# Square-sums moved from ScalarE to VectorE in every third block of an RMS-norm with SiLU

## The chip, the cores and the metric

The kernel runs on one core of a Trainium2 chip. The metric is device time in microseconds (us) of one execution; lower is better. A run also leaves a profile of one execution, whose span is about 2 us shorter than the device time.

## The reference

```python
x      # [8, 1024, 2048] float32
gamma  # [2048] float32
rms = np.sqrt(np.mean(x ** 2, axis=-1, keepdims=True) + eps)
out = gamma * x / rms
return (out * (1 / (1 + np.exp(-out)))).astype(np.float32)
```

The input of 67.1 MB is read once and an output of the same size is written once.

## The kernel before

The 8192 rows are taken in 16 blocks. A block is 4 MB: 128 partitions, each with J = 4 rows of 2048 numbers. Six buffers hold blocks; a block is loaded, worked on in place, and stored from the same buffer. Loads are issued from ScalarE's queue, stores from SyncE's.

```python
def sums(b, after_first=()):
    ss = small.tile([P, J], f32, name="ss")
    na = J // 2                                   # the line that is changed
    for j in range(na, J):
        nc.vector.tensor_tensor_reduce(           # L67: square-sum of row j on VectorE
            out=junk_v, in0=row(b, j), in1=row(b, j), scale=1.0, scalar=0.0,
            op0=ALU.mult, op1=ALU.add, accum_out=ss[:, j:j + 1])
    for j in range(na):
        nc.scalar.activation(out=junk_a, in_=row(b, j), func=ACT.Square,   # L71: the same on ScalarE
                             accum_out=ss[:, j:j + 1])
        if j == 0:
            for s in after_first:
                load(s)                           # L55: a later block's load
    rms = small.tile([P, J], f32, name="rms")
    nc.scalar.activation(out=rms, in_=ss, func=ACT.Sqrt, scale=1.0 / d, bias=eps_t)   # L77
    ...

def finish(b, halves=False):
    for j in range(J):
        nc.vector.scalar_tensor_tensor(...)       # L87: row j times 1/rms times gamma
        if j % 2:
            ...
            nc.scalar.activation(..., func=ACT.Silu)   # L91: two rows at once
            if halves:
                nc.sync.dma_start(...)            # L93: half a store, last block only

for b in range(1, last - 1):                      # blocks 0 and 1 come ahead of this loop
    sums(b + 1, after_first=[b + 3] if BUFS <= b + 3 < nblk else [])
    finish(b)
    store(b)                                      # L96
    invert(b + 1)                                 # L82
finish(last - 1)
store(last - 1)
sums(last)
invert(last)
finish(last, halves=True)
```

## Time and profile before

| | before |
|---|---|
| device time, median of 3 runs | 317.31 us (317.24 to 317.36) |
| VectorE (DVE) busy | 223.6 us, 71% of the span |
| ScalarE (ACT) busy | 223.7 us, 71% |
| moved by DMA | 134.24 MB, 426 GB/s over the span |

The page's chain of work that ended last, by engine and then by line, and two of its groups of instructions (operation, what is written and read, count; busy us, mean ns of one; idle before, and what ended it):

```profile
DMA 65%; DVE 18%; ACT 10%; issue 2%; DVEq 1%; ACTq 0%
DMA xt<-in_x_dram 65%; DVE xt L87 13%; ACT xt L91 6%; DVE junk_v L67 4%; ACT junk_a L71 2%; ACT L77 2%; DVEq L161 1%; ACT L91 0%; ACT rms L77 0%; DVE rstd L82 0%; DVE ss L67 0%; DVEq L67 0%; ACTq L77 0%
...
L67 DVE CUSTOM_DVE_ANT_0 junk_v<-xt 128x2048 f32<-128x2048 f32 x32 | 73.6, 2299 | 56.6 <-DMA xt<-in_x_dram 55.9
L71 ACT ACTIVATE junk_a<-xt 128x2048 f32<-128x2048 f32 x32 | 60.1, 1879 | 26.7 <-DMA xt<-in_x_dram 26.2
```

Two thirds of the chain are loads on their way, and both groups of square-sums, the work that the change moves, stand idle mainly until a load lands. The chain can't show that the DMA engines are full; the DMA row of the page does.

### The profile page before, as it was taken

The numbers are of one execution on the slowest core, as the hardware profiler recorded it, in microseconds if no ns is written. First come the engines' busy times: TensorE is split into PE (matmuls) and PEld (weight loads), VectorE is DVE, ScalarE is ACT, GpSimd is POOL, SyncE is SP. The second block draws the span as 40 slices with busy tenths as digits, with TensorE's granted clock in tenths as the row PEclk, the third lists the DMA queues.
The fourth block names the chain that finished last, engine by engine and source line by source line (L and its number), as shares of the span: only waits on it lengthen the run. The fifth ranks groups of instructions, "written<-read, shape, count | busy, mean of one in ns | idle before, by whom it ended". The sixth has DMA issues, their size and how long they took to land.

```text
span 315.1 us, 438 instructions
## 1 busy us (share of the span) xinstructions
PE 2.1 (1%) x8; PEld 0.5 (0%) x8; DVE 223.6 (71%) x147; ACT 223.7 (71%) x144; POOL 0.2 (0%) x4
## 2 busy tenths in 40 slices
PE   0200000000000000000000000000000000000000
PEld 0000000000000000000000000000000000000000
DVE  0679499999295692957939488493984929994920
ACT  1357958999768677686676776766867668779550
POOL 0000000000000000000000000000000000000000
DMA  8999999999999999999999999999999999999997
GB/s 334 408 458 408 391 458 408 458 408 458 408 459 408 459 408 453 412 458 412 453 412 453 420 445 424 445 420 445 428 437 428 441 433 433 441 424 441 424 418 314
DMA packets 4762, 134.24 MB, mean 426 GB/s; under 512 B 532, under 2 KB 532, under 8 KB 536
## 3 DMA queue, kind: packets, MB, share of 16 engines
q10 hardware_dynamic: 2304, 67.11, 49.8%
q1 hardware_dynamic: 2456, 67.12, 49.4%
q14 instruction: 2, 0.02, 0.0%
HBM read 67.12 MB, written 67.11 MB: 426 GB/s over the span
## 4 chain that ended last, share of the span: by engine, by line
DMA 65%; DVE 18%; ACT 10%; issue 2%; DVEq 1%; ACTq 0%
DMA xt<-in_x_dram 65%; DVE xt L87 13%; ACT xt L91 6%; DVE junk_v L67 4%; ACT junk_a L71 2%; ACT L77 2%; DVEq L161 1%; ACT L91 0%; ACT rms L77 0%; DVE rstd L82 0%; DVE ss L67 0%; DVEq L67 0%; ACTq L77 0%
## 5 line engine op out<-in xcount | busy, mean ns | idle before, releaser
L87 DVE SCALAR_TENSOR_TENSOR xt<-xt,rstd,g 128x2048 f32<-128x2048 f32 x64 | 146.2, 2347 | 0.1
L91 ACT ACTIVATE xt<-xt 128x4096 f32<-128x4096 f32 x32 | 115.5, 3616 | 39.2 <-DVE xt L87 39.2
L67 DVE CUSTOM_DVE_ANT_0 junk_v<-xt 128x2048 f32<-128x2048 f32 x32 | 73.6, 2299 | 56.6 <-DMA xt<-in_x_dram 55.9
L71 ACT ACTIVATE junk_a<-xt 128x2048 f32<-128x2048 f32 x32 | 60.1, 1879 | 26.7 <-DMA xt<-in_x_dram 26.2
L77 ACT ACT_TABLE_LOAD x15 | 19.2, 1283 | 9.9 <-DVE ss L67 9.9
L91 ACT ACT_TABLE_LOAD x15 | 19.2, 1283 | 0.3
L82 DVE RECIPROCAL rstd<-rms 128x4 f32<-128x4 f32 x16 | 2.8, 173 | 10.8 <-ACT rms L77 10.8
L111 DVE COPY g<-junk_v 128x2048 f32<-128x2048 f32 x1 | 2.3, 2292 | 9.3 <-PE junk_v L109 9.3
L71 ACT ACTIVATION_READ_ACCUMULATOR junk_a<-xt 128x1 f32 x32 | 6.0, 186 | 0.0
L77 ACT ACTIVATE rms<-ss,eps_t 128x4 f32<-128x4 f32 x16 | 4.8, 297 | 1.3 <-DVE ss L67 1.1
L67 DVE DVE_READ_ACCUMULATOR2_ANT ss<- 128x1 f32 x32 | 4.5, 141 | 0.0
L104 ACT ACT_TABLE_LOAD x1 | 1.3, 1283 | 3.8 <-issue 3.8
L109 PE MATMUL junk_v<-grow,ones 1*128 1x512 f32 x8 | 2.1, 1132 | 8.1 <-DMA grow<-in_gamma_dram 8.1
L102 DVE MEMSET ones<- 128x128 f32 x1 | 0.2, 165 | 0.8 <-PEq L147 0.8
L109 PEld LDWEIGHTS junk_v<-grow,ones 1*128 1x128 f32 x8 | 0.5, 306 | 8.1 <-issue 8.1
L104 ACT ACTIVATE junk_a<-ones 128x1 f32<-128x1 f32 x1 | 0.2, 175 | 0.0
L147 POOL MEMSET const-bfloat16-1.0<- 128x1 bf16 x1 | 0.1, 101 | 0.0
L147 POOL MEMSET const-uint8-127<- 128x1 uint8 x1 | 0.1, 101 | 0.0
L147 POOL MEMSET const-float32-0.0<- 128x1 f32 x1 | 0.1, 98 | 0.2 <-issue 0.2
L147 POOL MEMSET const-float32-1.0<- 128x1 f32 x1 | 0.1, 98 | 0.0
L103 DVE MEMSET eps_t<- 128x1 f32 x1 | 0.1, 59 | 0.0
## 6 DMA issues: line engine op xcount, KB each, us to landing
xt<-in_x_dram ACTq DMA_DIRECT2D x16, 4096.0 KB, 38.7
out_dram<-xt SPq DMA_DIRECT2D x15, 4096.0 KB, 34.6
out_dram<-xt SPq DMA_DIRECT2D x2, 2048.0 KB, 9.0
grow<-in_gamma_dram SPq DMA_DIRECT2D x1, 8.0 KB
```

Source lines behind the costliest of these rows:

```text
L67: nc.vector.tensor_tensor_reduce(out=junk_v, in0=row(b, j), in1=row(b, j), scale=1.0, scalar=0.0, op0=ALU.mult, op1=ALU.add, accum_out=ss[ ...
L71: nc.scalar.activation(out=junk_a, in_=row(b, j), func=ACT.Square, accum_out=ss[:, j:j + 1])
L77: nc.scalar.activation(out=rms, in_=ss, func=ACT.Sqrt, scale=1.0 / d, bias=eps_t)
L82: nc.vector.reciprocal(out=rstd, in_=rmss.pop(b))
L87: nc.vector.scalar_tensor_tensor(out=row(b, j), in0=row(b, j), scalar=rstds[b][:, j:j + 1], in1=g, op0=ALU.mult, op1=ALU.mult)
L91: nc.scalar.activation(out=blocks[b][:, cols], in_=blocks[b][:, cols], func=ACT.Silu)
L102: nc.vector.memset(ones, 1.0)
L104: nc.scalar.activation(out=junk_a[:, 0:1], in_=ones[:, 0:1], func=ACT.Square)
L109: nc.tensor.matmul(junk_v[:, c * w:(c + 1) * w], ones[k:k + 1, :], grow[k:k + 1, :], start=True, stop=True)
L111: nc.vector.tensor_copy(out=g, in_=junk_v)
L147: nc = _bacc.Bacc("TRN2", target_bir_lowering=False, num_devices=1)
L161: with _tile.TileContext(nc) as tc:
```

## The change

VectorE takes three of the four square-sums in blocks 2, 5, 8, 11 and 14, and ScalarE one. It relieves ScalarE, which also carries the table loads, the SiLU and the issue of loads.

```diff
         ss = small.tile([P, J], f32, name="ss")
-        na = J // 2
+        na = 1 if b % 3 == 2 else 2
         for j in range(na, J):
```

## The prediction

> **What bounds the kernel now.** I read the busy shares of the page first, then its 40 slices, then the waits, and last the timeline of the end of the span. The page:
>
> ```profile
> span 315.1 us, 438 instructions
> PE 2.1 (1%) x8; PEld 0.5 (0%) x8; DVE 223.6 (71%) x147; ACT 223.7 (71%) x144; POOL 0.2 (0%) x4
> ...
> DMA  8999999999999999999999999999999999999997
> ...
> HBM read 67.12 MB, written 67.11 MB: 426 GB/s over the span
> ```
>
> Neither VectorE nor ScalarE is full: both are at 71%, and evenly loaded. The DMA row is 9 in every slice but the first and the last. Between 66 and 240 us the windows view gives a DMA share of 1.00 at 434 GB/s. The 134.24 MB of the program at 434 GB/s take 309.3 us; the other 5.8 us of the span are starting and landing. The span is that of moving bytes, and the change moves none.
>
> The waits say the same from the other side:
>
> ```profile
> DVE junk_v L67 <- DMA xt<-in_x_dram: 55.9, 11, 5.5
> ACT xt L91 <- DVE xt L87: 39.2, 28, 3.6
> ACT junk_a L71 <- DMA xt<-in_x_dram: 26.2, 11, 7.9
> ```
>
> (Columns: us in total, times, longest.) From block 5 to block 14 VectorE stands 5.5 us in front of each block's square-sums until the block has landed. That is the room that the change may fill for nothing. How far ahead the two queues run is in the page's list of issues:
>
> ```profile
> xt<-in_x_dram ACTq DMA_DIRECT2D x16, 4096.0 KB, 38.7
> out_dram<-xt SPq DMA_DIRECT2D x15, 4096.0 KB, 34.6
> ```
>
> Blocks follow each other every 19.36 us (the square-sums of block 13 start at 240.28, those of block 14 at 259.66 by the timeline). A load takes 38.7 us from issue to landing, so it stands a whole block (19.3 us) behind another load; a store takes 34.6 us and stands 15.2 us in its queue. A store issued some us later therefore still finds its queue full.
>
> Two stretches are different. At the start the engines run without waiting for loads; at the end VectorE and ScalarE run one chain up to the last store. The end, by the timeline:
>
> ```profile
> 259.66 2.30 DVE L67 CUSTOM_DVE_ANT_0 junk_v<-xt 128x2048 f32<-128x2048 f32 x1 [5.54 <-DMA xt<-in_x_dram]
> ...
> 264.27 9.13 DVE L87 SCALAR_TENSOR_TENSOR xt<-xt,rstd,g 128x2048 f32<-128x2048 f32 x4
> ...
> 300.39 4.86 SPq L93 DMA_DIRECT2D out_dram<-xt  x2
> 301.27 3.62 ACT L91 ACTIVATE xt<-xt 128x4096 f32<-128x4096 f32 x1 [0.91 <-DVE xt L87]
> ```
>
> Block 14 lands at 259.55. From there: its sums, the scaling of blocks 13 and 14, the sums of 15, its scaling, and two half stores issued at 300.39 and 304.90. The reader is to see that this chain hangs on the landing of block 14, and that block 14 is a changed block (14 mod 3 = 2).
>
> **What the Trainium skill says.** "DMA: Bandwidth & Descriptors", section "Where 436 GB/s comes from", gives 435 GB/s as the fabric ceiling of a core's DMA; the trace has 434 in mid-span, so it agrees and nothing is left to win there. The same page, "Issuing engines are not separate DMA queues", says that transfers issued from different engines run on the same 16 DMA engines and interleave: the trace agrees, with 33.52 MB of loads and 33.55 MB of stores between 85 and 240 us. "VectorE: DVE Perf Modes", section "The TRN2 errata", gives (N+151)/0.96 ns for an fp32 tensor-tensor add, 2291 ns at 2048; the square-sum here measures 2299. "ScalarE: Activation LUTs", section "What ACT_TABLE_LOAD costs", gives 186 + 0.833 N ns for an ACTIVATE with immediate scale and bias, 1892 at 2048, and 1283 for a table load; the trace has 1879 and 1283.
>
> **The change part by part.** Blocks 2, 5, 8, 11 and 14 are changed; block 15 is not. In each, one square-sum goes from ScalarE to VectorE.
> - VectorE gains 5 x (2299 + 141) ns = 12.2 us of busy time and reaches 235.8 us (75%). Start to start a square-sum costs 2.39 us (259.66 to 262.05), since its accumulator read overlaps: 5 x 2.39 = 12.0 us of engine time.
> - ScalarE loses 5 x (1879 + 186) ns = 10.3 us and falls to 213.4 us (68%).
> - The listing of instruction order shows 31 table loads on ScalarE, as before, and nothing moved on the queue of stores.
>
> Where these lie:
> - Blocks 5, 8, 11: VectorE's wait of 5.5 us becomes 3.1 for the following block. The store behind is issued 2.4 us later, with 15.2 us in hand. Worth 0.
> - Block 2, at the start. VectorE has no wait there. Its sums run from 38.35 to 43.10; then block 1 is scaled and its last SiLU ends at 55.75, where store 1 is issued. All of that moves by 2.39 us, to 58.14. But the store queue is empty there: store 0 landed at 56.2 (32.69 + 23.5), and the first large packets of store 1 appear at about 59. While no stores run, loads have the whole rate instead of half: in the extra 2.39 us they gain 2.39 x 434/2 KB/ns = 0.52 MB, which at the shared rate of 217 GB/s is 2.39 us again. So I expect blocks 5 to 15 to land 2.4 us **earlier**, and stores of blocks 1 and after to land as much later. No byte is lost.
> - Block 14, at the end: one more square-sum, +2.39 us on the chain to the last stores. Set against the earlier landing (257.2), the chain from 264.3 on stands where it stood: 2.39 - 2.39 = 0. The last two stores are issued at about 300.4 and 304.9 again.
>
> Sum: 0. Saved ScalarE time is worth nothing: no path that sets the end passes through the sums it loses (in block 14 the chain runs over VectorE's).
>
> If the landing doesn't come earlier, the last stores are issued at 302.8 and 307.3. In the trace the first packets of the half store issued at 300.39 appear at 303.25, when store 14's large packets have just ended; an idle queue starts moving about 0.9 us after an issue (first load: 0.73 to about 1.6). So the margin is 303.25 - 300.39 - 0.9, about 2.0 us, and of 2.39 some 0.4 us would show, at most about 1.5 if starting takes 2 us there.
>
> **The rivals.**
> - The end of the span takes the full price of block 14's extra sum: +2.4 us (0.8%), 319.7. For it: that sum is on the chain of waits. Against: the DMA is busy to the end (shares 0.91 to 1.08 from 290 to 313 us), so the last stores queue for their turn.
> - VectorE becomes the bound. Against: per changed block it needs about 4 x 2.30 + 3 x 2.39 + 0.2 = 16.5 us of the 19.36.
> - A new wait in the issue of loads: load b+3 needs store b-3 landed. Store 3 landed at 118.2 and load 9 was issued at 124.0; loads 2.4 us earlier and stores 2.4 later leave 1.0 us of 5.8. If negative, ScalarE stands a little in front of an issue; the load still has a whole load ahead of it, so 0.
> - Faster, because ScalarE is relieved or the engines better balanced: they were even before and neither bounds. 0 at best, some tenths from noise of DMA packing.
>
> **Range and chances.** Before is 317.31 us, its three runs within 0.12. I add 0.1 for the chance of a small hole before the last stores: 317.4 us. The range, 316.9 to 318.3, goes from an unlikely gain of 0.4 to a hole of 1. A gain of 2% is 6.3 us, more than all of the span's 5.8 us outside the transfer: not possible. A loss of 2% needs over 6 us on the chain at the end, which gets 2.4. Chances: faster 0.003, same 0.985, slower 0.012.
>
> **What would show it right or wrong.** In the changed profile VectorE at about 236 us and ScalarE at about 213; DMA row unchanged; VectorE's total wait for loads down from 55.9 to about 42 to 50; blocks 5 to 14 landing about 2.4 us earlier (block 14 at 257.2, not 259.55); last stores issued near 300.4 and 304.9. It would be wrong if the last stores came 2.4 us later and the DMA row showed a gap before them, if a wait of ScalarE's queue for stores grew to more than a block's time, or if the rate in mid-span changed with the mix of loads and stores.

## The result, and the profile after

| | before | after |
|---|---|---|
| median of 6 runs each | 317.29 us (317.21 to 317.36) | 317.18 us (316.91 to 318.33) |
| VectorE busy | 223.6 us | 235.3 us |
| ScalarE busy | 223.7 us | 213.3 us |

The ratio of after to before is 1.0001, 95% interval 0.9986 to 1.0016: the same. A ratio here is the mean time of one kernel's fast runs over that of the other's of the same rounds, so not quite the ratio of the medians above.

The page after, head and DMA row:

```profile
span 315.6 us, 438 instructions
...
PE 2.1 (1%) x8; PEld 0.5 (0%) x8; DVE 235.3 (75%) x157; ACT 213.3 (68%) x134; POOL 0.2 (0%) x4
...
DMA  8999999999999999999999999999999999999997
```

Ten instructions left ScalarE and ten came to VectorE (five square-sums, each with its accumulator read), and the DMA row is the one of before. The waits after (us in total, times, longest):

```profile
DVE junk_v L67 <- DMA xt<-in_x_dram: 44.4, 11, 5.5
ACT xt L91 <- DVE xt L87: 39.2, 28, 3.6
ACT L77 <- DVE ss L67: 23.7, 11, 5.3
ACT junk_a L71 <- DMA xt<-in_x_dram: 19.0, 7, 8.0
```

VectorE's wait for loads fell from 55.9 to 44.4 us, by 11.5: about what five square-sums of 2.39 us take. ScalarE only exchanged work for waiting: it stands 23.7 us for VectorE's sums ahead of the square root's table load, where it stood 9.9, and gave up 10.4 us of busy time. So the work moved into one engine's idle time and left idle time on the other.

The begin of block 5 before, and then four moments of the timeline after: block 5, block 14 (its first square-sum, then the scaling of block 13) and the last stores (columns: start, duration, engine, line, operation):

```profile
85.39 2.30 DVE L67 CUSTOM_DVE_ANT_0 junk_v<-xt 128x2048 f32<-128x2048 f32 x1 [5.52 <-DMA xt<-in_x_dram]
```

```profile
83.37 2.30 DVE L67 CUSTOM_DVE_ANT_0 junk_v<-xt 128x2048 f32<-128x2048 f32 x1 [1.27 <-DMA xt<-in_x_dram]
...
257.69 2.30 DVE L67 CUSTOM_DVE_ANT_0 junk_v<-xt 128x2048 f32<-128x2048 f32 x1 [5.54 <-DMA xt<-in_x_dram]
...
264.70 9.14 DVE L87 SCALAR_TENSOR_TENSOR xt<-xt,rstd,g 128x2048 f32<-128x2048 f32 x4
...
300.81 4.86 SPq L93 DMA_DIRECT2D out_dram<-xt  x2
```

Block 5 is begun at 83.37, where before it was 85.39. Block 14 is begun at 257.69, where before it was 259.66: 1.97 us earlier. Its one more square-sum costs 2.4 us, and the last stores are issued at 300.81 instead of 300.39. They land 9.0 us after their issue, as before.

### The profile page after: what moved, and what is told of

It is laid out like the page before. It is cut to its first block, busy times and chain, and to the rows that moved or that the text cites. A ratio compares the mean times of both kernels' runs of the same rounds, so it can differ in the third digit from the quotient of the medians.

```text
span 315.6 us, 438 instructions
## 1 busy us (share of the span) xinstructions
PE 2.1 (1%) x8; PEld 0.5 (0%) x8; DVE 235.3 (75%) x157; ACT 213.3 (68%) x134; POOL 0.2 (0%) x4
## 3 DMA queue, kind: packets, MB, share of 16 engines
q1 hardware_dynamic: 2456, 67.12, 49.4%
## 4 chain that ended last, share of the span: by engine, by line
DVE 43%; DMA 41%; ACT 9%; issue 3%; DVEq 1%; another core or an unknown queue 0%; ACTq 0%
DMA xt<-in_x_dram 41%; DVE xt L87 27%; DVE junk_v L67 15%; ACT xt L91 6%; ACT junk_a L71 1%; ACT L77 1%; DVEq L161 1%; DVE ss L67 0%; ACT rms L77 0%; DVE rstd L82 0%; DVEq L67 0%; ACTq L77 0%
## 5 line engine op out<-in xcount | busy, mean ns | idle before, releaser
L67 DVE CUSTOM_DVE_ANT_0 junk_v<-xt 128x2048 f32<-128x2048 f32 x37 | 85.0, 2298 | 45.1 <-DMA xt<-in_x_dram 44.4
L71 ACT ACTIVATE junk_a<-xt 128x2048 f32<-128x2048 f32 x27 | 50.6, 1875 | 19.4 <-DMA xt<-in_x_dram 19.0
L77 ACT ACT_TABLE_LOAD x15 | 19.2, 1283 | 23.8 <-DVE ss L67 23.7
L67 DVE DVE_READ_ACCUMULATOR2_ANT ss<- 128x1 f32 x37 | 5.2, 141 | 0.0
L71 ACT ACTIVATION_READ_ACCUMULATOR junk_a<-xt 128x1 f32 x27 | 5.0, 186 | 0.0
```

The costliest lines, as they stand in the source:

```text
L67: nc.vector.tensor_tensor_reduce(out=junk_v, in0=row(b, j), in1=row(b, j), scale=1.0, scalar=0.0, op0=ALU.mult, op1=ALU.add, accum_out=ss[ ...
```

## The experiments

Eleven kernels were run; all gave the reference's result. The four of the first group ran on one chip, five rounds each.

**The changed kernel again.** No edit.

> The changed kernel once more, on the chip of its parts, for its spread. Both theories: 317.2 us, ratio to before within 0.4% of 1; the last two stores issued near 300.8 and 305.3 as in its first trace, or up to 1 us around it, since its six runs spread over 1.4 us and those of before over 0.15.

Measured: 317.2 us median, but 316.82 to 320.72, against 317.13 to 317.49 of before (9 runs); ratio 0.9998 (0.9985 to 1.0012). The run of 320.72 was the profiled one, so its trace can be read; it is taken up at the end of this section. The expectation on the spread was too narrow.

**Block 2 alone.**

```diff
-        na = J // 2
+        na = 1 if b == 2 else 2
```

> Only block 2 is changed. Theory (store 1 comes 2.4 us later into an empty store queue, so loads gain that time): block 5 lands about 2.0 us earlier than before (near 83.3, not 85.3), block 14 near 257.6, and the last two stores are issued about 2 us earlier than before (298.4 and 302.9); the time stays within 0.3 us of 317.3 because the DMA has the same bytes to move. Rival (the early landing comes from elsewhere in the change, or from chance): block 14 lands at 259.5 as before, last store at 304.9.

Measured: 317.05 us, ratio 0.9999 (0.9986 to 1.0011). The timeline has block 14 begun 3.5 us earlier than before (256.18 against 259.66), and the last stores issued at 296.92 and 301.4:

```profile
256.18 2.30 DVE L67 CUSTOM_DVE_ANT_0 junk_v<-xt 128x2048 f32<-128x2048 f32 x1 [5.52 <-DMA xt<-in_x_dram]
...
296.92 4.86 SPq L93 DMA_DIRECT2D out_dram<-xt  x2
```

They land 12.4 us after issue instead of 9.0. A block has landed when the last of the 16 DMA engines is done with it. By the packet records (explained below) the median engine ended load 14 2.4 us earlier than before (255.17 against 257.56 us), as expected; the last engine ended it 3.5 us earlier (255.72 against 259.18), since the engines lie closer together in this trace. So block 2 by itself brings all later blocks forward, by more than expected, and the time stays: the stores only stand longer in their queue.

**Blocks 5, 8 and 11 alone.**

```diff
-        na = J // 2
+        na = 1 if b in (5, 8, 11) else 2
```

> Only blocks 5, 8 and 11 are changed. Theory: nothing moves: block 14 lands at 259.5, last stores issued at 300.4 and 304.9, VectorE's wait for loads down by about 7 us in total to 49, time 317.3 within 0.2. Rival (the mix of work in mid-span shifts landings or the DMA's rate): landings off by over 0.5 us.

Measured: 317.0 us, ratio 0.9994 (0.9981 to 1.0006). Block 14 is begun at 260.06, 0.4 us later than in the trace of before, and the last stores are issued 0.4 later; VectorE's wait for loads is 49.4 us in total. As the theory had it: the middle part fills a wait.

**Block 14 alone.**

```diff
-        na = J // 2
+        na = 1 if b == 14 else 2
```

> Only block 14 is changed. Theory: block 14 lands at 259.5 as before, the last two stores are issued 2.39 us later (302.8 and 307.3), of which the queue hides about 2.0: time longer by 0.4 us, at most 1.5. Rival 1 (the end pays the full price): longer by 2.4 us, 319.7. Rival 2 (hidden wholly): 317.3.

Measured: 316.97 us, ratio 0.9992 (0.9979 to 1.0004). The last stores:

```profile
302.64 4.86 SPq L93 DMA_DIRECT2D out_dram<-xt  x2
```

They are issued 2.25 us later than before and land 6.7 us after issue instead of 9.0: at the same moment. The extra sum is hidden to within 0.1 us: by the packet records the engines stand idle 0.08 us on average, 0.2 at most, before these stores, so this delay is about the whole reserve. Rival 2 was right here, and the 0.4 us of the theory were not there.

**Block 14, with two sums repeated.** How much does the end hide? The next four kernels ran on one chip, three rounds each.

```diff
-        na = J // 2
-        for j in range(na, J):
+        na = 1 if b == 14 else 2
+        for j in [*range(na, J)] + ([3, 3] if b == 14 else []):
```

> Only block 14 is changed, and VectorE does two of its square-sums of row 3 again there (same result), so the chain at the end is 3 x 2.39 = 7.2 us longer and no more bytes move. The run with one extra sum hid all of its 2.39 us. Theory (the store queue hides what it has in hand, about 2.4 us, and no more): last stores issued 7.2 us later (307.6 and 312.1), time longer by 7.2 - 2.4 = 4.8 us, 322.0 (321.3 to 322.8), with a hole in the DMA row before the last stores. Rival 1 (the end is free of VectorE): 317.2. Rival 2 (full price): 324.4.

Measured: 320.55 us, ratio 1.0111 (1.0092 to 1.0131). Busy time in three stretches near the end (PE, PEld, DVE, ACT and POOL, then clock, DMA share and GB/s):

```profile
301.00:303.00 2.00, 0.00 (x0) 0.00 (x0) 2.00 (x2) 0.03 (x1) 0.00 (x0) 1.00 1.22 524
303.00:307.00 4.00, 0.00 (x0) 0.00 (x0) 4.00 (x2) 3.59 (x1) 0.00 (x0) 1.00 0.00 0
307.00:309.00 2.00, 0.00 (x0) 0.00 (x0) 0.46 (x1) 1.50 (x1) 0.00 (x0) 1.00 0.94 393
```

From 303 to 307 no byte moves while VectorE and ScalarE work: this is the hole that the small change didn't make. The last stores are issued at 306.61, 6.2 us later than before (block 14 landed 0.9 us earlier in this trace); the span is 3.6 us longer. So about 2.6 us are hidden and the rest is paid. The time lies below the expected 321.3 to 322.8; the early landing and the somewhat larger reserve account for most of it. Both rivals fall.

**Block 2, with two sums repeated.**

```diff
-        na = J // 2
-        for j in range(na, J):
+        na = 1 if b == 2 else 2
+        for j in [*range(na, J)] + ([3, 3] if b == 2 else []):
```

> Only block 2 is changed, with the same two repeated sums, so store 1 is issued 7.2 us later than before (near 62.9). Theory: loads have the empty store queue's share for that time, blocks land earlier (block 14 by 5 to 8 us, at 252 to 254.5 instead of 259.5), and the time stays at 317.2 within 0.6, since bytes bound it. Rival (delay at the start is passed on to the end, or the later stores hold up the issue of loads so that the load queue runs dry): block 14 lands no earlier than before, time over 319.

Measured: 317.25 us, ratio 1.0001 (0.9984 to 1.0018). Block 14 is begun at 253.86, 5.8 us earlier than before, and the last two stores land 15.9 us after issue. (The trace is of a run of 318.1 us, the slowest of the four.) A delay of 7.2 us at the start costs nothing. It does make a new wait, the one named as a rival in the prediction, by the waits of this run:

```profile
DVE junk_v L67 <- DMA xt<-in_x_dram: 43.5, 9, 5.5
ACT junk_a L71 <- DMA out_dram<-xt: 37.7, 7, 5.4
```

ScalarE stands before seven blocks until a store has landed and its buffer is free for the next load; that too is hidden.

**Three sums on VectorE in every block.**

```diff
-        na = J // 2
+        na = 1
```

> VectorE takes three square-sums in every block: VectorE busy 223.6 + 16 x 2.44 = 262.7 us (83%), ScalarE 223.7 - 16 x 2.07 = 190.6. Per block VectorE needs 9.13 + 3 x 2.39 + 0.2 = 16.5 of 19.36 us. Theory: still the DMA's time, 317.2 within 0.6. Rival (balance matters): longer by the 33 us of moved work's excess or some part, over 319.

Measured: 322.17 us (321.88 to 323.12), ratio 1.0157 (1.0139 to 1.0175). The theory failed. The page:

```profile
PE 2.1 (1%) x8; PEld 0.5 (0%) x8; DVE 260.9 (81%) x179; ACT 190.9 (60%) x112; POOL 0.2 (0%) x4
...
DMA  8999999999999999999999999999999999999995
```

VectorE still waits for loads, 25.1 us in all. The DMA row is as full as before, with a share of 1.00 between 110 and 250 us, and yet 427 GB/s are moved there instead of 432. The same bytes take longer.

**Four sums on VectorE in blocks 2 to 14.**

```diff
-        na = J // 2
+        na = 0 if 2 <= b <= 14 else 2
...
+        if na == 0:
+            for s in after_first:
+                load(s)
         rms = small.tile([P, J], f32, name="rms")
```

> VectorE takes all four square-sums in blocks 2 to 14, and the load is issued ahead of the square root instead of after ScalarE's first sum. VectorE needs 9.13 + 4 x 2.39 + 0.2 = 18.9 us per block of 19.36: it can't make good what it loses at the start (3 blocks x 4.8 us = 14.3). Theory: VectorE works without a break from block 2 on and becomes the bound: scaling of block 13 ends near 284 instead of 273.4, last store near 315 instead of 304.9, time 317.2 + 10.4 - 2.4 = 325 (322 to 327). Rival (DMA still hides it): 317.2 within 1.

The edit also moves the issue of the later load ahead of the square root, since ScalarE has no sum left behind which to issue it. Measured: 320.6 us (319.9 to 322.5), ratio 1.0112 (1.0076 to 1.0147); the trace is of the run of 322.5 us, the slowest. VectorE is busy 173.08 of the 174 us between 66 and 240 us, as expected; but a block takes it 18.5 us (the load issues come 18.51 apart), not 18.9, so it makes up ground, and the last stores are issued at 305.82 and 310.34, not 315. They land 9.1 us after issue, as before (9.0): on most engines the store ahead of them is still moving then, and those that are done stand idle a little (a share of 0.84 from 306 to 307, by the packet records). VectorE is thus at most a small part of what the end waits for; the expected mechanism fell. Again the rate is lower, 426 GB/s between 110 and 250 us.

**What lowers the rate.** Two theories were left: a busier VectorE slows transfers (B), or it matters how loads and stores stand to each other in time (A). For A the trace's records of single DMA packets were counted, each with start, duration, queue and size. A block is moved by 128 packets of 32 KB, 8 for each of the 16 engines, and ends with 16 records of 4 bytes, taken here as one from each engine (the records don't name the engine). "Distance" below is from the end of a load to the end of the nearest store in mid-span (median of each one's 16 end records); as stores follow each other without a gap, that is also when the next store begins; it is positive where the store comes after the load.

Packet durations in the table are means of those that start in a stretch of 130 us in mid-span, from about 105 us; shifted by some us, the stretch gives 1241 to 1250, 1254 to 1261 and 1251 to 1257 for the three slow kernels, and the same numbers for the others. The last three rows are the runs described next. DVE is its busy time between 66 and 240 us, the rate that between 110 and 250 us:

```
kernel                 store 1    distance  32KB load  32KB store  rate    DVE     median
                       issued us  us        ns         ns          GB/s    us      us
before                 55.8       -4.9      1213.1     1213.5      432     124.2   317.3
block 2                58.2        0.0      1213.1     1214.2      432     129.4   317.05
changed kernel         58.2       -0.4      1213.1     1213.6      433     135.2   317.2
block 2, two repeats   63.0       +7.6      1213.5     1213.3      433     136.4   317.25
three in every block   60.1       +2.4      1240.6     1215.7      427     152.0   322.2
four in 2 to 14        60.4       +2.5      1253.9     1215.2      426     173.1   320.6
three in 3 to 15       55.8       -4.9      1213.0     1213.4      432     147.6   317.9
9 blocks, a repeat     55.9       -4.9      1213.0     1213.7      433     143.1   317.6
block 2, one repeat    60.4       +2.5      1251.0     1216.1      426     128.8   321.7
```

The two slow ones above the last three rows have VectorE busiest, and also the same distance, one that no other has. The following three, on one chip, set one against the other.

**Three sums in blocks 3 to 15**, so VectorE is nearly as busy as with three in every block, but the first stores come as before.

```diff
-        na = J // 2
+        na = 1 if b >= 3 else 2
```

> VectorE takes three square-sums in blocks 3 to 15, but not in 0 to 2, so the first stores come as before (store 1 at 55.8). VectorE in mid-span is as busy as in the run with three in every block, which took 322.2 us with a mid-span rate near 427 GB/s. Theory A (that loss came from how load and store stand to each other in time: there a store began 2.4 us after a load, each block; before it ended 4.9 us ahead): here the distance is as before, rate 433, time 317.3 within 0.6. Theory B (a busier VectorE slows the transfers): rate near 427 again, time 320 to 322.

Measured: 317.86 us, ratio 1.0015 (1.0001 to 1.0030). The rate between 110 and 250 us is 432 GB/s, and the distance is that of before. The last stores are issued at 302.73, 2.3 us later than before, and land 7.4 us after issue. The 0.5 us are within what was expected and were not followed further.

**One sum repeated in blocks 5 to 13**, with ScalarE's work unchanged.

```diff
-        na = J // 2
-        for j in range(na, J):
+        na = 2
+        for j in [*range(na, J)] + ([3] if 5 <= b <= 13 else []):
```

> The kernel before with one square-sum of row 3 repeated on VectorE in blocks 5 to 13 (same result); ScalarE's work is unchanged. Theory A (distance in time of load and store): as before, rate 433 and 317.2 us within 0.4. Theory B (VectorE's work slows the transfers): rate below 430 and 319 or more.

Measured: 317.6 us, ratio 1.0010 (0.9992 to 1.0027). Rate 433.

**Block 2, with one sum repeated.**

```diff
-        na = J // 2
-        for j in range(na, J):
+        na = 1 if b == 2 else 2
+        for j in [*range(na, J)] + ([3] if b == 2 else []):
```

> Only block 2 is changed, with one repeated sum, so store 1 comes 4.8 us later than before (near 60.5), as late as in the two slow runs (60.1 and about 60.6); VectorE is no busier than before in mid-span. Theory A: stores begin some 2.4 to 4 us after a load; if it is 2.4, load packets are lengthened each block as in the slow runs, rate near 427, time 319.5 to 322. Theory B: rate 433, time 317.2 within 0.6. If the distance comes out otherwise than 2.4, the run doesn't tell.

Measured: 321.7 us (321.84, 321.78, 321.61, and one of 318.86), ratio 1.0116 (1.0074 to 1.0158). The stretch from 110 to 250 us in four runs: one sum repeated in block 2, three in blocks 3 to 15, one repeated in blocks 5 to 13, and before (columns as above):

```profile
110.00:250.00 140.00, 0.00 (x0) 0.00 (x0) 97.41 (x64) 99.53 (x64) 0.00 (x0) 1.00 1.00 426
```

```profile
110.00:250.00 140.00, 0.00 (x0) 0.00 (x0) 117.22 (x81) 86.02 (x52) 0.00 (x0) 1.00 1.00 432
```

```profile
110.00:250.00 140.00, 0.00 (x0) 0.00 (x0) 117.62 (x82) 99.92 (x66) 0.00 (x0) 1.00 1.00 433
```

```profile
110.00:250.00 140.00, 0.00 (x0) 0.00 (x0) 101.07 (x66) 101.62 (x67) 0.00 (x0) 1.00 1.00 432
```

The slow one has VectorE least busy, 97.4 us, and those with 117 us run at full rate. Theory B falls.

Delay as such isn't it either: repeating none, one or two sums in block 2 gives 317.05, 321.7 and 317.25 us (each on another chip, beside its own before). The wait of load issues for stores isn't it: 13.0 us in the slow run with one repeat, but 37.7 in the run with two at full rate, and none in the other two slow kernels.

What the three slow kernels share is a store that begins 2.4 to 2.5 us after a load has ended, which is the time of two 32 KB packets (2 x 1.213). There the packet records show 20-odd load packets per block lengthened, for 2 to 4 us from the begin of each store. In the run with one repeat these sum to about 5 us per block over 16 engines, so some 0.3 us a block on the average engine, and the 16 engines drift apart: from the first to the last engine's end of a load it takes 1.5 us in load 5 and 3.8 in load 15.

A last store has landed only when the slowest engine is done, and its end records give the whole loss of this trace: they come at 314.98 (first), 316.56 (median) and 318.73 us (last), before at 313.10, 313.29 and 313.87. The last one is 4.9 us later, as is the end of the span: 3.3 us are lost on the median engine, the rest is drift.

The distance was not set by itself: it followed from the delay of store 1, which is issued at 60.1 to 60.4 us in all three slow kernels and in no other, and one trace was taken of each. That the distance, and not something else which goes with that delay, lengthens the packets is therefore argued (the long packets lie at the begin of the stores), not shown. Why load packets take longer there and not at 0, 7.6 or -4.9 us, the runs don't tell; neither do they tell why one run in four of that kernel lost only 1.5 us.

The run of 320.72 us of the changed kernel resembles these but is not the same: between 70 and 110 us it moved 421 GB/s with lengthened *store* packets, at a distance of -1.2 to -1.6 us; from 150 us on, at -1.2, it was at full rate. Its loss is almost all drift: the end records of its last store have their median at 314.32 us and the last at 317.66, against 313.83 and 314.34 in the first trace of the changed kernel. What set it off stays open.

## Why the prediction was right

- **The bound** was the bytes. Shown: more VectorE work in blocks 5 to 13 left the time as it was (ratios 0.9994 and 1.0010), and so did a start delayed by 7.2 us (1.0001); no run of any kernel took less than 316.8 us.
- **The busy times** came out at 235.3 and 213.3 us, predicted 235.8 and 213.4; the wait of VectorE for loads at 44.4, within 42 to 50.
- **Blocks 5, 8, 11: 0.** Shown by their own run, 317.0 us.
- **Block 2: all blocks land 2.4 us earlier.** The mechanism was right, the size not exact: 2.0 us in the changed kernel, 3.5 with block 2 alone. On the median engine load 14 ended 1.8 and 2.4 us earlier: with block 2 alone the expected gain was there to the tenth, and the prediction had left out that the engines don't end together. In the changed kernel's trace store 0 itself took 25.0 us to land instead of 23.5, so the store queue ran empty later; whether that is the difference was not tested.
- **Block 14: +2.4 us, cancelled by the earlier landing.** It came to 2.4 - 2.0 = 0.4 us later stores. That was hidden, but so it would have been without block 2: block 14 alone cost nothing. The step that was mis-sized is the reserve at the end. I put it at 2.0 us, with some 0.4 us to show; the runs show a shift of 2.25 us hidden to within 0.1, and 2.6 us hidden of 6.2. The working took 303.25 us for the end of store 14; the packet records have it at 303.37 on the first engine and 304.14 on the last, and an idle queue moved its first packets 0.83 us after the issue in the run with two repeats in block 14 (306.61 to 307.44). From these I estimate a reserve of 2.2 us on the first engine and 2.9 on the last.
- **Of the rivals,** the full price at the end (319.7) fell with the run of block 14 alone. The wait of load issues for stores did not appear in the changed kernel; with three times the delay it did, 37.7 us long, and cost nothing, as argued. VectorE as the bound did not come either, even with four sums a block.
- **The spread** was underrated. The number was taken from three runs of before within 0.12 us. The changed one gave 316.82 to 318.33 in eleven runs, about the whole range, and 320.72 in one, far outside it. The rate in mid-span was named as what would make the prediction wrong, but given no weight; the experiments show that a delay of 2.4 us more in the same place of block 2 would have done it: that is the run with one sum repeated in block 2, at 321.7. That the change's own delay missed this place was luck: nothing in the prediction tells the two delays apart.

## What to carry to other kernels

In a kernel like this one, whose DMA row is full and whose engines both wait for loads, moving work between the engines moves waits, and the one thing to work out is what the change does at the two ends of the span, where queues are empty or draining: a late store at the start lets loads run ahead, and a late store at the end is free as long as its predecessor is still moving. Measure that reserve by lengthening the chain until a hole shows in the DMA row. And when a kernel that only moves bytes gets slower with its DMA row still full, compare the GB/s of mid-span and how loads and stores stand to each other in time before blaming the engine that got busier.

## What the Trainium skill lacked or had wrong

- "DMA: Bandwidth & Descriptors", section "Issuing engines are not separate DMA queues", says that transfers from different engines interleave, which the traces show. It doesn't say that the rate can then differ with how two streams stand to each other in time (here set by the delay of one store): 432 to 433 GB/s at distances of -4.9, 0.0 and +7.6 us, 426 to 427 at +2.4 to +2.5, with 32 KB load packets of 1241 to 1254 ns on average instead of 1213.
- The same page, section "Latency and other measured facts", gives about 0.6 us to the first byte for transfers issued from SyncE or ScalarE. On idle queues the traces agree if one counts from the end of the issuing instruction: the first load's packets appear 0.6 us after it (1.11 to 1.74; 1.0 us after its begin at 0.73), those of the last stores in the run with two repeats in block 14 0.5 us after it (306.94 to 307.44). What is lacking is the figure behind a full load queue: store 0, issued at 32.69, has its first packets at 37.09, 4.4 us later, and store 1 of the kernel before 3.5 us later (55.77 to 59.28). No page has that.
